# An encoder of a Hyena/GLA layer and an RWKV-7 layer: earlier conditioning, and two value projections in the keys stage

## The chip, the cores and the metric

The kernel runs on one core of a Trainium2 chip (trn2). The metric is the device time of one execution in microseconds (us). Shown before is the median of three runs; one further execution was taken by the hardware profiler, and all rows come from that one.

Engines: PE is TensorE (PEld its weight loads), DVE is VectorE, ACT is ScalarE, POOL is GpSimd, and SP is SyncE, whose queue issues nearly all transfers here.

## The reference

Two layers over a sequence of 256 tokens with 2048 features, all in float32. Each layer has a mixer and a squared-ReLU MLP (2048 to 8192 and back), and each of these four parts ("mix", "f0", "tm", "f1") is conditioned by a vector `c`: `silu(c) @ ada_w + ada_b` gives a shift, a scale and a gate of 2048 numbers each. The first mixer is Hyena beside a gated linear attention; the second ("tm") is RWKV-7 time mixing.

```python
def adaln(x, c, norm_g, ada_w, ada_b):
    m = jax.nn.silu(c) @ ada_w + ada_b
    shift, scale, gate = jnp.split(m[:, None, :], 3, axis=-1)
    return rmsnorm(x, norm_g) * (1.0 + scale) + shift, gate
...
def rwkv7_block(...):
    xx = 0.5 * (hp[:, :-2] + hp[:, 2:]) - h
    xr, xw, xk, xv, xa, xg = [h + xx * mu[j] for j in range(6)]
    r = heads(xr @ w_r); k = heads(xk @ w_k); v = heads(xv @ w_v)
    ...
    for d in range(2):      # both directions: decays, keys, then a scan over the tokens
        ...
        state_out = state_out + o_d
    ...
    return o @ w_o
...
        x = x + gate * y
        h, gate = adaln(x, c, ffn_norm_g[layer], ffn_ada_w[layer], ffn_ada_b[layer])
        x = x + gate * sqrelu_mlp(h, ffn_w1[layer], ffn_w2[layer])
```

The scan is written in chunks of 64 tokens. 32 heads of 64 features make 16 pairs, and four pairs (512 features) a block.

## The kernel before

**Weights.** Every large product is split into three matmuls: a weight tile of 128 x 2 x 512 is loaded by SP (`load`, L488), ACT casts it to a high part and DVE subtracts to get the low part (`split`, L464), and `prod` (L507) issues high x high, high x low and low x high. Each MLP loads 256 such tiles, in the order `w1`, `w2`, `w1`, `w2`, 64 at a time.

**Conditioning as background work.** A third (shift, scale or gate) of one of the four parts is 32 halves. A half is one load of 512 KB into pool `wp` of six tiles (`ada_load`, L313, up to five ahead) and one DVE product with a running sum (`ada_half`, L362). Each weight load adds `rate / 2` to an account, and whenever it reaches one, a half is done (`tick`, L501). In the first MLP the rate is `RF0`, and the account begins at -12. `ada_load` names the order: the current part's gate, then shift and scale of all parts. In the RWKV layer the rate is 0 and the halves are done by `bg_gen` in the loop over pairs; the gate of `tm` is done there, and `spread_gate` spreads it over the partitions at the end of that loop.

**The RWKV layer** (`rwkv`, L1104) has stages. First the six mixes of the input are made; `xk` stays on chip in tiles `xk`, the mixes for `r` and `v` are written to memory and read back, two chunks of 128 features at a time, by `stream` (L999), with a ring of tiles `x`. Second, the keys stage: four rounds over blocks `n`. In each, `rwkv_keys` of four pairs runs in two lanes, woven with the projections `mains`: `k` and `r` of the next blocks, and in round 4 the value block 0. A projection (`rwkv_linear`, L1025) has 16 steps of 12 matmuls, so 192 matmuls, and 8 weight tiles. Value tiles stay on chip. Third, the loop over pairs `p` (L1236): `weave` runs, side by side, the chain of pair `p` (`pair_chain`: four steps, each three rounds of small matmuls with copies by DVE and ACT between), the preparation of the next pair (`pair_prep`), the tail of an earlier one (`pair_tail`), `MT[p]` steps of `main`, the inversion of small triangles, or `BG[p]` conditioning halves. `main` (`work`, L1211) is the rest of the values, blocks 1 to 3, and then the output projection (`rwkv_out`), whose steps wait for finished pairs (`tails`). `M0 + M1` steps of it stand before the first chain: the text calls that stretch the transition. What of the output projection is left follows the last chain.

The order of instructions on each engine's queue is set by a planner with a timeline of its own, within the dependencies and priorities that the program gives; `paced` holds a projection's matmul behind a chain's.

Of the kernel before, what the change touches and what calls it, by code (L numbers as in the profile page):

```python
# [9 lines left out]
F32 = mybir.dt.float32  # L10
# [17 lines left out]
PT = ("0111111", "0111")  # L28
RHY, RGL, RWO, RF0, RF1 = 2.4, 2, 0.6, 1.2, 0.8
HA, HB, HN, HT = 1000, 1000, 0, 0  # L30
LG, MK, XS, TB, DU, RP, IB, L1, MP, AP = 2, 7, 4, 0, -8.0, 1, 3, 0, 3, 5
W1, W2 = 1, 1
BG, IV, CH, MT, B0, B1, M0, M1, LD = (10, 10, 10, 10, 10, 10, 10, 10, 10, 5, 5, 5, 5, 5, 5, 5, 5, 5), 12, 7, (5, 5, 5, 5, 5, 5, 5, 5, 5, 5, 5, 2, 3, 2, 3, 2, 3, 2), 3, 14, 6, 6, 6
PK, PF = 8, 3
RH, ZZ = (0, 2.4, 2, 2), 0
# [178 lines left out]
class Build:  # L214
# [21 lines left out]
    def run(self):  # L236
        nc, ctx, A = self.nc, self.ctx, self.A
        self.const = self.pool(ctx, "const")
        self.wp = self.pool(ctx, "wp", bufs=6)
        self.due, self.rate, self.turn, self.hold, self.starting = 0.0, 0.0, 0, None, False  # L240
        self.cut, self.casts, self.wq = None, [], None
        self.small = self.pool(ctx, "small", bufs=2)
        self.tmp = self.pool(ctx, "tmp", bufs=4)
        self.gstack = ctx.enter_context(ExitStack())
        self.open_gate()
        self.wstack = ctx.enter_context(ExitStack())
        self.open_work()
        self.mm = self.pool(ctx, "mm", bufs=4, space=PSUM)
        self.q = {"sp": nc.sync, "act": nc.scalar, "pool": nc.gpsimd}[QM]
        self.pstack = ctx.enter_context(ExitStack())  # L250
        self.open_ps(4)
        self.xstack = ctx.enter_context(ExitStack())
        self.ada_left = {(s, i): 2 * KT for s in self.stages if s in SUBS for i in range(3)}
        self.ada_next, self.ada_sum, self.ada_out, self.ada_done = [], {}, {}, {}
        self.label = self.stages[0]
        if self.stages[0] != "mix":
            self.start()
            self.load_x()
        for s in SUBS:
            if s in self.stages:  # L260
                self.label = s
                self.rate = RF0 if s == "f0" else RF1
                if s[0] == "f":
                    self.ffn(s)
                elif s == "mix":
                    self.mix()
                else:
                    self.rwkv()
        self.final()
# [43 lines left out]
    def ada_load(self):  # L313

        left, s = self.ada_left, self.label
        todo = [(s, 2)] if not left.get((s, 0)) and not left.get((s, 1)) else []
        if s == "mix" and left.get((s, 0)):
            todo = [(s, 0 if left[s, 0] % 2 or left[s, 0] == left[s, 1] else 1)]
        if self.starting:
            todo = [("mix", i) for i in range(2)] if not todo or todo[0][1] == 2 else todo  # L320
        else:
            todo += [(q, i) for q in SUBS for i in range(2)]
        for u in todo:
            if left.get(u):
                w = self.t(self.wp, [P, D // 2], "w")
                i, j = divmod(2 * KT - left[u], 2)
                self.nc.sync.dma_start(w, self.A["ada_" + u[0]][u[1] * KT + i][:, j])
                left[u] -= 1
                return *u, i, w, j
# [134 lines left out]
    def split(self, a, hi, lo, eng=None):  # L464
        c = self.nc.scalar.copy(hi, a)  # L465
        d = (eng or self.nc.vector).tensor_tensor(lo, a, hi, ALU.subtract)  # L466
        if eng is None:
            self.cut = d.ins
            self.casts = [c.ins]

# [17 lines left out]
    def load(self, name, n, i, pools):  # L488

        self.turn += 1  # L490
        w = self.t(pools[self.turn % len(pools)], [P, 2, NB], "w")
        src = self.A[name][n, i // 2][:, i % 2 * 2 : i % 2 * 2 + 2]
        if self.wq is None:
            self.dma = self.nc.sync.dma_start(w, src).ins
        else:
            with self.tc.issue_after(self.casts[-1]):
                self.wq.dma_start(w, src)
        self.tick(self.rate / 2)
        return w
# [499 lines left out]
    def stream(self, name, n, src, tiles):  # L999
# [4 lines left out]
        def ahead(i):  # L1004
            if isinstance(src, list):
                x = src[i // 4][:, 2 * i % 8 : 2 * i % 8 + 2]
            else:
                x = self.t(self.xt, [P, 2, 2, T], "x", bufs=self.xb, dt=F32R)
                nc.sync.dma_start(x.bitcast(F32), src[:, 2 * i : 2 * i + 2])
            if 2 * (i + PF) < tiles:  # L1010
                w.append(self.load(name, n, i + PF, [self.wp]))
            v = [self.t(self.ws, [P, 2, NB], t, dt=F32R) for t in ("wh", "wl")]
            self.split_weights(w[i], v)
            return x, v
# [89 lines left out]
    def rwkv(self):  # L1104
# [6 lines left out]
        self.ab = [tc.dram_tile([P, 2304 + 8], F32, name=f"ab{p}") for p in range(16)]  # L1111
        self.nd = [tc.dram_tile([P, 2, 1024], F32, name=f"nd{b}") for b in range(4)]
        self.rx = [tc.dram_tile([4, 32, 1024], F32, name=f"rx{b}") for b in range(4)]
        self.rt = [tc.dram_tile([4, 32, 1024], F32, name=f"rt{b}") for b in range(4)]
        self.npt, self.marks, self.tails, self.lag = 0, [], 0, L1
        self.pr = PR
        with ExitStack() as st:
# [4 lines left out]
            nc.vector.tensor_scalar(self.ksc[:, 1, :], self.v("ka"), -0.5, 1.0, ALU.mult, ALU.add)  # L1122
            vp = self.pool(st, "vp", reuse_waits="tile")
            vt = {}

            def values(n, pool):
                def tiles():
                    vt[n] = self.t(pool, [P, 4, T], "v")
                    return vt[n]

                yield from self.rwkv_linear("rw_v", n, 3, tiles)

            st1 = st.enter_context(ExitStack())
            self.open_linear(st1, 3, W1, 3)
            xk = self.pool(st1, "xk", reuse_waits="tile")
            self.xd[2] = [self.t(xk, [P, 8, 2, T], f"xk{i}", dt=F32R) for i in range(2)]
            rk = self.pool(st1, "rk", reuse_waits="tile")
# [15 lines left out]
            mains = [g for n in range(4) for g in (keys(n), self.rwkv_linear("rw_r", n, 0, lambda n=n: kr[n][0]))]  # L1153
            mains = self.in_turn(mains + [values(0, vp)], LD)
            with ExitStack() as st2:
# [11 lines left out]
                self.xstack.close()  # L1167
                self.rate, self.wq = 0.0, None
                mixes = self.spill_mixes(h, xx)
# [5 lines left out]
            with st1:  # L1175
                p1 = self.pool(st1, "p1", reuse_waits="tile")
                for n in range(4):
# [16 lines left out]

                    self.weave((self.take(mains, 34), 34 if n < 3 else 17), (lane(0), 21), (late(), 24), (self.invert(n - 1) if 0 < n <= IB else None, 34))
            with ExitStack() as st1:
                self.open_linear(st1, 2, W2, 3)
                p2 = self.pool(st1, "p2", reuse_waits="tile")
# [12 lines left out]
                def work():  # L1211
                    for n in range(1, 4):
                        yield from values(n, (vp, p2)[n % 2])
                    if PK:
# [10 lines left out]
                def spread_gate(pool):  # L1225
                    r, g = self.need("tm", 2), self.t(pool, [P, 4, T], "v")
                    for i in range(2):
                        self.spread(r, 2 * len(self.gates) + i, g[:, 2 * i : 2 * i + 2, :].rearrange("p a t -> p (a t)"))
                    self.gates.append(g)

                main = work()
                for _ in self.take(main, M0):
                    pass
                self.weave((self.pair_prep(p2, Z[0], vt[0][:, 0, :]), 12), (self.take(main, M1), M1))
                chains, self.gates = {}, []
                for p in range(18):  # L1236
# [3 lines left out]
                    if p < 15:  # L1240
                        nx = self.pair_prep(p2, Z[p + 1], vt[(p + 1) // 4][:, (p + 1) % 4, :])
                    if p == 17:
                        self.npt = None
                        spread_gate(vp)
                    if p < 14:
# [21 lines left out]
                for n in range(4):  # L1267
# [9 lines left out]
                    self.residual("tm", n, pts[n])  # L1277
        self.wq = None
        self.open_gate()
        self.open_work()  # L1280

    def spill_mixes(self, h, xx):
        for j in (2, 0, 3):
            for k in range(0, KT, 2):
# [3 lines left out]
                if j == 2:  # L1288
                    x = self.xd[2][k // 8][:, k % 8 : k % 8 + 2]
                else:  # L1290
                    x = self.t(self.hp, [P, 2, 2, T], "xs", bufs=2, dt=F32R)
# [153 lines left out]
    def pair_load(self, rp, p):  # L1445
        nc = self.nc
        b, pb = p // 4, p % 4
        z = {"p": p}
        z["ar"] = ar = self.t(rp, [P, 2, 2, T], "ar", bufs=2)
        z["bk"] = bk = self.t(rp, [P, 2, 4, P], "bk", bufs=2)  # L1450
# [20 lines left out]

    def pair_prep(self, rp, z, v):

# [4 lines left out]
        X, Tt, N = z["X"], z["T"], z["N"]  # L1478
        z["v"] = v
        z["S"], z["BKT"], z["M"] = {}, [], []  # L1480
# [245 lines left out]
```

## Time and profile before

| | us |
|---|---|
| median of 3 runs | 3051.21 (3048.9 to 3052.1) |
| profiled execution | 3047.34 |
| its span, first to last instruction | 3045.3 |
| first MLP, starts of the first and the last weight split | 648.7 and 1372.5 |
| second MLP, the same (the RWKV layer lies between) | 2300.5 and 3025.8 |

A row of the windows gives, for a stretch of the span, the busy time of each engine with its number of instructions, the granted clock of TensorE as a share of 2.4 GHz, the mean busy share of the 16 DMA engines, and GB/s. A row by line gives line, engine, operation, tiles written and read, shapes, count, busy time, mean of one in ns, and the idle time just before with what ended it. A row of waits says who waited for whom: total, times, longest. Busy time of PE comes from modelled ends of matmuls that overlap.

### The profile page before, as it was taken

To read this page: it belongs to the slowest core of one execution; us is meant where nothing else is said; L and a number is where in the kernel's file an instruction comes from. 1 tells how busy PE (TensorE), PEld (TensorE's weight loads), DVE (VectorE), ACT (ScalarE), POOL (GpSimd) and SP (SyncE) were. 2 spreads that over 40 slices of the span, in tenths; PEclk is the share of its full clock that TensorE was granted. 3 is DMA by queue.
4 is the path that set the end of the run, shared out by engine and by line. 5 is a ranking of instruction groups with operands and counts; after the bars stand their busy time and mean duration, and the time that the engine had idled before them with its cause. 6 is when DMAs were issued, how large, how long until landed. Compare 5 with 4: busy or idle time off the path is not lost. (4 is left out here: it accounts for less than half of the span.)

```text
span 3045.3 us, 52042 instructions
## 1 busy us (share of the span) xinstructions
PE 2871.4 (94%) x20308; PEld 2488.7 (82%) x20308; DVE 2122.1 (70%) x3126; ACT 1301.6 (43%) x1947; POOL 522.2 (17%) x574
## 2 busy tenths in 40 slices
PE   6999989999999999997999878999998999999998
PEld 2678776789988999886888777777778998899986
DVE  7899866657777788787768875775646776455454
ACT  3233334444443444443466542334445443344443
POOL 1211200011100011004354541322322110001000
PEclk9999999999999999998999987999999999999999
DMA  9978777747898988984987788997545777555552
GB/s 328 326 271 284 243 262 263 247 154 244 287 308 306 304 290 290 313 297 158 323 264 249 266 258 226 301 300 208 149 149 194 245 252 272 193 186 183 202 193 93
DMA packets 279970, 752.30 MB, mean 247 GB/s; under 512 B 73081, under 2 KB 99577, under 8 KB 278572
## 3 DMA queue, kind: packets, MB, share of 16 engines
q1 hardware_dynamic: 279148, 745.38, 73.1%
q8 instruction: 159, 2.61, 0.3%
q10 hardware_dynamic: 576, 3.60, 0.3%
q14 instruction: 87, 0.71, 0.1%
HBM read 706.08 MB, written 42.80 MB: 246 GB/s over the span
## 5 line engine op out<-in xcount | busy, mean ns | idle before, releaser
L466 DVE TENSOR_TENSOR f_wl<-f_w,f_wh 128x1024 fp32r<-128x1024 f32 x512 | 630.8, 1233 | 444.3 <-ACT f_wh L465 433.4
L465 ACT CAST f_wh<-f_w 128x1024 fp32r<-128x1024 f32 x512 | 538.0, 1052 | 748.4 <-PE f_mm L512 315.8
L511 PE MATMUL f_mm<-f_h,f_wh 128*128 128x256 f32 x2048 | 579.5, 283 | 0.0
L510 PE MATMUL f_mm<-f_h,f_wh 128*128 128x256 f32 x2048 | 579.5, 283 | 0.0
L512 PE MATMUL f_mm<-f_h,f_wl 128*128 128x256 f32 x2048 | 579.1, 283 | 0.0
L511 PE MATMUL f_mm<-f_wl,f_hid 128*128 128x512 f32 x1024 | 398.6, 389 | 1.1 <-DVE f_wl L466 1.1
L512 PE MATMUL f_mm<-f_wh,f_hid 128*128 128x512 f32 x1024 | 398.5, 389 | 0.0
L511 PEld LDWEIGHTS f_mm<-f_h,f_wh 128*128 128x128 f32 x2048 | 393.2, 192 | 0.1
L510 PEld LDWEIGHTS f_mm<-f_h,f_wh 128*128 128x128 f32 x2048 | 393.0, 192 | 0.1
L512 PEld LDWEIGHTS f_mm<-f_h,f_wl 128*128 128x128 f32 x2048 | 392.9, 192 | 0.0
L510 PE MATMUL f_mm<-f_wh,f_hid 128*128 128x512 f32 x1024 | 357.9, 389 | 0.0
L362 DVE SCALAR_TENSOR_TENSOR mix_w<-mix_w,mix_s 128x1024 f32<-128x1024 f32 x175 | 219.8, 1265 | 77.0 <-DMA mix_w<-in_ada_f 52.5
L466 POOL TENSOR_TENSOR f_hid<-f_u,f_hid 128x512 fp32r<-128x512 f32 x64 | 98.0, 1531 | 990.6 <-ACT f_hid L465 988.2
L362 DVE SCALAR_TENSOR_TENSOR f_w<-f_w,mix_s 128x1024 f32<-128x1024 f32 x174 | 233.6, 1345 | 2.6 <-DMA f_w<-in_ada_f 2.6
L511 PEld LDWEIGHTS f_mm<-f_wl,f_hid 128*128 128x128 f32 x1024 | 192.2, 188 | 41.3 <-DVE f_wl L466 1.7
L512 PEld LDWEIGHTS f_mm<-f_wh,f_hid 128*128 128x128 f32 x1024 | 192.3, 188 | 39.8
L510 PEld LDWEIGHTS f_mm<-f_wh,f_hid 128*128 128x128 f32 x1024 | 192.2, 188 | 39.7
L466 DVE TENSOR_TENSOR tm_wl<-tm_w,tm_wh 128x1024 fp32r<-128x1024 f32 x128 | 164.4, 1287 | 85.8 <-ACT tm_wh L465 81.6
L465 ACT CAST mix_wh<-mix_w 128x1024 fp32r<-128x1024 f32 x114 | 119.4, 1050 | 201.2 <-PE mix_mm L512 86.3
L510 PE MATMUL tm_mm<-tm_x,tm_wh 128*128 128x256 f32 x512 | 161.2, 316 | 12.3 <-DMA tm_x<-mix 10.8
L465 ACT CAST tm_wh<-tm_w 128x1024 fp32r<-128x1024 f32 x128 | 133.4, 1046 | 86.7 <-PE tm_mm L511 60.3
L466 DVE TENSOR_TENSOR mix_wl<-mix_w,mix_wh 128x1024 fp32r<-128x1024 f32 x114 | 142.4, 1254 | 38.8 <-ACT mix_wh L465 38.7
(456 smaller groups left out, 5494.6 us busy)
## 6 DMA issues: line engine op xcount, KB each, us to landing
f_w<-in_w SPq DMA_DIRECT2D x512, 512.0 KB, 5.1
f_w<-in_ada_f SPq DMA_DIRECT2D x125, 512.0 KB, 5.6
mix_w<-in_ada_mix SPq DMA_DIRECT2D x96, 512.0 KB, 6.2
mix_w<-in_w_in SPq DMA_DIRECT2D x80, 512.0 KB, 5.0
mix_w<-in_ada_f SPq DMA_DIRECT2D x64, 512.0 KB, 5.2
tm_x<-mix SPq DMA_DIRECT2D x64, 512.0 KB, 5.8
f_w<-in_ada_tm SPq DMA_DIRECT2D x49, 512.0 KB, 5.8
mix_w<-in_w_out SPq DMA_DIRECT2D x32, 512.0 KB, 4.6
```

Source lines behind the costliest of these rows:

```text
L362: V.scalar_tensor_tensor(w, w, 1.0, self.s[:, j * (D // 2) : (j + 1) * (D // 2)], ALU.mult, ALU.mult, accum_out=a[:, j, i : i + 1])
L465: c = self.nc.scalar.copy(hi, a)
L466: d = (eng or self.nc.vector).tensor_tensor(lo, a, hi, ALU.subtract)
L510: mm(out, lhsT=l[0], rhs=r[0], start=start, stop=False)
L511: mm(out, lhsT=l[0], rhs=r[1], start=False, stop=False)
L512: mm(out, lhsT=l[1], rhs=r[0], start=False, stop=stop)
```

## The change

The gate of `tm` may now be conditioned in the first MLP (`EARLY`), whose rate rises from 1.2 to 1.5. Two value blocks instead of one (`NV`) are projected in the keys stage, in round 4; for them the mix for `v` is loaded once, into tiles that take the places of `xk`. Blocks 2 and 3 stream it as before. Every value block is written to memory, and each pair loads its own part two pairs ahead. The ring of `x` in the pairs' stage has two tiles instead of three. `BG` and `MT` are single numbers, and `VL` is the weight of the projections in round 4. A queue `wq` that was never set is taken out.

```diff
-RHY, RGL, RWO, RF0, RF1 = 2.4, 2, 0.6, 1.2, 0.8
+RHY, RGL, RWO, RF0, RF1 = 2.4, 2, 0.6, 1.5, 0.8
...
-BG, IV, CH, MT, B0, B1, M0, M1, LD = (10, 10, 10, 10, 10, 10, 10, 10, 10, 5, 5, 5, 5, 5, 5, 5, 5, 5), 12, 7, (5, 5, 5, 5, 5, 5, 5, 5, 5, 5, 5, 2, 3, 2, 3, 2, 3, 2), 3, 14, 6, 6, 6
-PK, PF = 8, 3
+BG, IV, CH, MT, B0, B1, M0, M1, LD = 3, 12, 7, 5, 3, 14, 6, 6, 6
+PK, PF, VL, NV, EARLY = 8, 3, 20, 2, (("f0", "tm"),)
...
-            todo += [(q, i) for q in SUBS for i in range(2)]
+            todo += [(q, i) for q in SUBS for i in range(3 if (s, q) in EARLY else 2)]
...
             if isinstance(src, list):
-                x = src[i // 4][:, 2 * i % 8 : 2 * i % 8 + 2]
+                x = src[i]
...
+        self.vd = [tc.dram_tile([P, 4, T], F32, name=f"vd{n}") for n in range(4)]
...
-            self.xd[2] = [self.t(xk, [P, 8, 2, T], f"xk{i}", dt=F32R) for i in range(2)]
+            resident = lambda: [self.t(xk, [P, 2, 2, T], f"xk{i}", dt=F32R) for i in range(KT // 2)]
+            self.xd[2] = resident()
...
-            mains = self.in_turn(mains + [values(0, vp)], LD)
+
+            def values(n, pool):
+                if n == 0:
+                    self.xd[4] = self.xd[3]
+                    spilt, self.xd[3] = self.xd[3], resident()
+                    for i, x in enumerate(self.xd[3]):
+                        nc.sync.dma_start(x.bitcast(F32), spilt[:, 2 * i : 2 * i + 2])
+                v = []
+
+                def tiles():
+                    v.append(self.t(pool, [P, 4, T], "gate", bufs=1 + (pool is not rk)))
+                    return v[0]
+
+                yield from self.rwkv_linear("rw_v", n, 3 if n < NV else 4, tiles)
+                nc.sync.dma_start(self.vd[n], v[0])
+
+            mains = self.in_turn(mains + [values(n, rk) for n in range(NV)], LD)
...
-                    self.weave((self.take(mains, 34), 34 if n < 3 else 17), (lane(0), 21), (late(), 24), (self.invert(n - 1) if 0 < n <= IB else None, 34))
+                    self.weave((self.take(mains, 34 if n < 3 else 17 * NV + 1), 34 if n < 3 else VL), (lane(0), 21), (late(), 24), (self.invert(n - 1) if 0 < n <= IB else None, 34))
             with ExitStack() as st1:
-                self.open_linear(st1, 2, W2, 3)
+                self.open_linear(st1, 2, W2, 2)
...
-                    for n in range(1, 4):
-                        yield from values(n, (vp, p2)[n % 2])
+                    for n in range(NV, 4):
+                        yield from values(n, p2)
...
-                    r, g = self.need("tm", 2), self.t(pool, [P, 4, T], "v")
+                    r, g = self.need("tm", 2), self.t(pool, [P, 4, T], "gate", bufs=2)
...
+        z["v"] = self.t(rp, [P, T], "v", bufs=6)
+        nc.sync.dma_start(z["v"], self.vd[b][:, pb, :])
         z["ar"] = ar = self.t(rp, [P, 2, 2, T], "ar", bufs=2)
...
-    def pair_prep(self, rp, z, v):
+    def pair_prep(self, rp, z):
...
-        z["v"] = v
+        v = z["v"]
```


## Rows read from the trace of the kernel before

**Rows 1.** The page: busy time per engine, then GB/s in 40 slices

```profile
PE 2871.4 (94%) x20308; PEld 2488.7 (82%) x20308; DVE 2122.1 (70%) x3126; ACT 1301.6 (43%) x1947; POOL 522.2 (17%) x574
...
GB/s 328 326 271 284 243 262 263 247 154 244 287 308 306 304 290 290 313 297 158 323 264 249 266 258 226 301 300 208 149 149 194 245 252 272 193 186 183 202 193 93
```

**Rows 2.** Windows of the MLPs: stretch, length, busy (instructions), clock, DMA, GB/s

```profile
840.00:1016.00 176.00, 176.00 (x805) 146.80 (x804) 136.14 (x179) 70.25 (x70) 4.87 (x2) 1.00 0.90 309
1016.00:1200.00 184.00, 184.00 (x1518) 183.22 (x1516) 146.53 (x171) 82.50 (x93) 20.59 (x14) 1.00 0.87 293
1200.00:1374.00 174.00, 174.00 (x789) 144.95 (x788) 137.27 (x175) 72.62 (x80) 2.89 (x2) 1.00 0.88 302
...
2670.00:2854.00 184.00, 184.00 (x1518) 183.26 (x1517) 97.49 (x82) 82.39 (x93) 20.77 (x14) 1.00 0.54 189
2854.00:3027.00 173.00, 173.00 (x783) 144.10 (x783) 91.54 (x84) 72.70 (x79) 2.97 (x2) 1.00 0.46 158
```

**Rows 3.** Windows of the RWKV layer, last a stretch of the second MLP

```profile
1664.00:1745.00 81.00, 71.99 (x590) 65.99 (x589) 65.11 (x118) 46.54 (x90) 38.88 (x49) 0.94 0.80 259
1745.00:1805.00 60.00, 49.19 (x425) 44.58 (x424) 50.37 (x102) 33.66 (x74) 26.80 (x48) 0.91 0.85 271
1805.00:1889.00 84.00, 68.44 (x599) 58.30 (x598) 43.74 (x97) 20.01 (x42) 16.52 (x32) 0.74 0.80 221
1889.00:2045.00 156.00, 149.40 (x1871) 124.84 (x1869) 117.11 (x249) 62.20 (x154) 39.77 (x65) 0.97 0.94 292
2045.00:2203.00 158.00, 156.77 (x2092) 121.27 (x2089) 95.48 (x219) 71.59 (x189) 51.28 (x83) 1.00 0.66 192
2203.00:2292.00 89.00, 86.12 (x601) 64.85 (x598) 46.45 (x76) 41.51 (x78) 23.55 (x22) 1.00 0.44 148
2540.00:2560.00 20.00, 18.88 (x90) 15.47 (x89) 17.32 (x27) 7.49 (x8) 0.00 (x0) 1.00 0.99 387
```

**Rows 4.** Windows of tile wh alone; DVE counts its splits

```profile
1664.00:1745.00 81.00, 51.55 (x248) 41.71 (x247) 18.78 (x16) 15.71 (x15) 0.94 0.80 259
1745.00:1805.00 60.00, 29.35 (x143) 24.32 (x143) 9.26 (x8) 8.26 (x8) 0.91 0.85 271
```

**Rows 5.** Stores of keys stage and pairs: duration min/median/max, first and last start

```profile
L1414 SPq DMA_DIRECT2D ab<-tm_bon x5: 319/374/570, 1745.6 to 1804.5; - x5
...
L1654 SPq DMA_DIRECT2D y_spill<-tm_o x5: 333/383/401, 1916.1 to 2036.7; - x5
...
L1654 SPq DMA_DIRECT2D y_spill<-tm_o x8: 343/550/1160, 2059.3 to 2202.0; - x8
```

**Rows 6.** Conditioning loads (line 327) of the first MLP, with time to landing

```profile
L327 SPq DMA_DIRECT2D f_w<-in_ada_f x93: 327/328/449, 692.6 to 1360.7; - x93
L327 SPq DMA_DIRECT2D f_w<-in_ada_tm x49: 327/328/653, 860.1 to 1081.6; - x49
...
DMA to landing us min/median/max: 3.5/5.7/7.9
```

**Rows 7.** Groups by line, 1374 to 2300 us: the conditioning's products

```profile
L362 DVE SCALAR_TENSOR_TENSOR tm_w<-tm_w,mix_s 128x1024 f32<-128x1024 f32 x35 | 44.1, 1265 | 13.4 <-DMA tm_w<-in_ada_tm 13.1
```

**Rows 8.** Groups by line, 840 to 1374 us: the same line

```profile
L362 DVE SCALAR_TENSOR_TENSOR f_w<-f_w,mix_s 128x1024 f32<-128x1024 f32 x120 | 157.1, 1310 | 2.2 <-DMA f_w<-in_ada_f 2.2
```

**Rows 9.** Windows of line 510 alone, early and late chains

```profile
1889.00:2045.00 156.00, 36.91 (x114) 21.92 (x114) 0.97 0.94 292
2045.00:2203.00 158.00, 25.05 (x58) 10.93 (x58) 1.00 0.66 192
```

**Rows 10.** Waits of PE in the transition, 1805 to 1889 us

```profile
PE tm_mm L510 <- DMA tm_x<-mix: 7.9, 2, 4.9
```

**Rows 11.** Loads of the stored mixes, 1640 to 2100 us

```profile
DMA to landing us min/median/max: 4.6/6.0/10.6
```

More of the change, by code (lines that the diff above doesn't have):

```diff
@@ L240, in run @@
         self.due, self.rate, self.turn, self.hold, self.starting = 0.0, 0.0, 0, None, False
-        self.cut, self.casts, self.wq = None, [], None
+        self.cut = None
         self.small = self.pool(ctx, "small", bufs=2)
@@ L464, in split @@
     def split(self, a, hi, lo, eng=None):
-        c = self.nc.scalar.copy(hi, a)
+        self.nc.scalar.copy(hi, a)
         d = (eng or self.nc.vector).tensor_tensor(lo, a, hi, ALU.subtract)
@@ L468, in split @@
             self.cut = d.ins
-            self.casts = [c.ins]
     def behind(self):
@@ L491, in load @@
         w = self.t(pools[self.turn % len(pools)], [P, 2, NB], "w")
[L492 to L497, printed above, removed]
+        self.dma = self.nc.sync.dma_start(w, self.A[name][n, i // 2][:, i % 2 * 2 : i % 2 * 2 + 2]).ins
         self.tick(self.rate / 2)
@@ L1122, in rwkv @@
             nc.vector.tensor_scalar(self.ksc[:, 1, :], self.v("ka"), -0.5, 1.0, ALU.mult, ALU.add)
[L1123 to L1131, printed above, removed]
             st1 = st.enter_context(ExitStack())
@@ L1167, in rwkv @@
                 self.xstack.close()
-                self.rate, self.wq = 0.0, None
+                self.rate = 0.0
                 mixes = self.spill_mixes(h, xx)
@@ L1233, in rwkv @@
                     pass
-                self.weave((self.pair_prep(p2, Z[0], vt[0][:, 0, :]), 12), (self.take(main, M1), M1))
+                self.weave((self.pair_prep(p2, Z[0]), 12), (self.take(main, M1), M1))
                 chains, self.gates = {}, []
@@ L1240, in rwkv @@
                     if p < 15:
-                        nx = self.pair_prep(p2, Z[p + 1], vt[(p + 1) // 4][:, (p + 1) % 4, :])
+                        nx = self.pair_prep(p2, Z[p + 1])
                     if p == 17:
                         self.npt = None
-                        spread_gate(vp)
+                        spread_gate(p2)
                     if p < 14:
@@ L1277, in rwkv @@
                     self.residual("tm", n, pts[n])
-        self.wq = None
         self.open_gate()
@@ L1288, in spill_mixes @@
                 if j == 2:
-                    x = self.xd[2][k // 8][:, k % 8 : k % 8 + 2]
+                    x = self.xd[2][k // 2]
                 else:
```

## The prediction

> **What bounds the kernel now.** I read the page first: TensorE (PE) is busy 94% of a span of 3045.3 us, VectorE (DVE) 70% [rows 1]. The profiled execution took 3047.34 us in all, 2.0 us of it outside the span and 3.9 us below the median of 3051.21. The sum below is made against 3047.34, and its difference is then put on the median. About 0.2%, 6 us, is what a measurement of this kernel can tell from no change.
>
> An average over three kinds of stage says little, so next come the windows of the stages. In the two MLPs PE is busy without a gap [rows 2]. One `w1` stretch (64 weight tiles) takes 184 us in the first MLP and 184 us in the second; one `w2` stretch takes 174 and 173 us. The first MLP does this with DMA at 0.87 to 0.90 of its time and the second with 0.46 to 0.54. So PE alone sets the pace of the first MLP; its DVE (78%) and its transfers lie beside it. That pace also gives the price of a matmul of 128x256: 184 us for 1518, 0.121 us each, at a granted clock of 1.00.
>
> The RWKV layer has three stages [rows 3]. The keys stage (up to 1805) runs four rounds of four pairs; beside each round stand projection blocks. Round 3, like rounds 1 and 2, has 16 weight splits, two blocks, and takes 81 us; round 4 has 8 splits, one block, and takes 60 us [rows 3, 4]. The last stores of rounds 3 and 4 confirm this: 1745.6 and 1804.5 [rows 5]. PE is idle for 10.8 us of the 60. Then comes a transition (1805 to 1889), in which the second value block is multiplied while PE is idle 15.6 us of 84 and has a granted clock of 0.74, for most of it the lower of the two levels. Last come the chains (1889 to 2203) and the rest of the output projection (to 2292), where PE is busy 149.4 of 156, 156.8 of 158 and 86.1 of 89 us. A pair takes (2036.7-1916.1)/4 = 30.2 us early and (2202.0-2059.3)/7 = 20.4 us later [rows 5].
>
> **The change part by part.**
>
> *Conditioning moved into the first MLP.* The first MLP loads 93 + 49 = 142 halves [rows 6], and the RWKV layer works through 35 more, all in the chains [rows 7]. With RF0 = 1.5 each of its 256 weight loads adds 0.75 to the account, which begins at -12: 256 x 0.75 - 12 = 180 halves, and 142 + 35 = 177 are wanted. All should fit, and nothing is left for the chains. In the MLP this adds 35 x 1.31 = 46 us of DVE [rows 8]. In a `w2` stretch of 176 us that is 64 x 0.15 = 9.6 halves or 13 us more, 149 of 176 us, 85%: still covered by PE. The traffic per weight load grows from 0.524 x 1.6 to 0.524 x 1.75 = 0.918 MB in 2.75 us, that is from a reckoned 305 GB/s (measured 309) to 334. A share of 0.90 for 309 GB/s makes 343 at full share, so the stretch would stand at about 0.97. What covers the transfers is the distance at which loads are issued: six tiles of `wp` at 0.75 + 1/7 tiles per load are 6.7 loads or 18 us ahead, against 5.7 us to landing [rows 6]. I take 0. The lower bound is 0 too, since PE waits for nothing here now. The upper bound: if no more than 328 GB/s came through, as in the best 76 us of the page's slices [rows 1], a load would take 0.918/0.328 = 2.80 us; against 2.72 in the `w2` stretches that is 0.08 us for each of 128 loads, 10 us; I say +12.
>
> *What that frees in the chains.* DVE loses 35 products of 1.265 us, 44.1 us, and 13.1 us in which it stood waiting for their transfers with chain work queued behind it [rows 7]. How much of these 57 us was on the path? Early pairs are 9.8 us longer than late ones. The projection matmuls beside them explain a part: early 3 x 114 of 0.121 us, 41 us in 156; late 3 x 58, nearly all twice as wide, some 38 us in 158 [rows 9], that is 8.0 us per early pair and 4.9 per late one. Clock explains about 1 us per pair (0.97 of 156 us). There remain some 5.7 us over five pairs, 28 us, for DVE, its waits and transfers at 0.94 of the time. Bounds 0 and -28. I take -10, nearer to nothing, because PE shows only 6.6 us of idle time in the 156.
>
> *One value block out of the chains, one more into the keys stage.* A block is 192 matmuls, 192 x 0.121 = 23 us of PE. Before, block 0 runs in round 4, block 1 in the transition, 2 and 3 in the chains; after, 0 and 1 run in round 4, 2 in the transition, 3 in the chains. Round 4 then has what rounds 2 and 3 have: 81 - 60 = +21 us. The lower bound is 23 - 10.8 = +12, if all its idle PE time is filled; the upper is +23. I take +20. The chains lose 23 us of PE work; where PE is that full the time falls by as much: -23. Bounds: -5 (if the wait between steps, not PE, sets the pace) and -23. The transition keeps one block, with its second-half `x` streamed through two buffers where there were three; PE waited 7.9 us there for `tm_x` [rows 10], which lands in 6.0 us [rows 11]. I put 0, bounds 0 and +5.
>
> *The input held on chip, the trip of the values through memory, the rest.* Blocks 0 and 1 share one load of 8 tiles instead of two, 4.2 MB less. The tiles take the places of the keys' input, so the eight loads wait for the last key block and come as one burst; behind them on SP's queue stand round 4's loads. 4.2 MB at that round's 271 GB/s are 15 us of transfer for a block that is needed at once only in its first tile: 0, bound +3. Four stores and 16 loads of values are added and 35 + 8 loads fall away, at 0.33 us of SP each [rows 6]; the queue gets shorter, and each load is issued two pairs (over 40 us) ahead: 0. BG and MT as constants and VL change only how the filling work is spread. The gate's spreading stays at the end.
>
> Sum: 0 - 10 + 20 - 23 = -13 us on 3047.34, about 3034; on the median 3038.
>
> **A rule against the reading.** The windows show weight loads busy 124.8 of 156 and 121.3 of 158 us in the chains, and 183.2 of 184 us in the `w1` stretch [rows 2, 3]. The Trainium skill (Perfetto Trace Analysis, "Identifying the Most-Contended Engine") says that matmul busy time is a poor measure of how near PE is to its limit and that the busy share of weight loads is a better one. By that rule the chains have a fifth of PE to spare. Its result is rival 1, and the rows do not exclude it.
>
> **Rivals.** *1, slower: the chains are set by their own steps.* If each pair is a sequence of small matmuls with copies between, and projection matmuls only fill gaps, then taking a block out gives the lower end, -5, and clearing DVE gives nothing, while round 4 still pays +20: +15, 3066 us. It decides once the pairs stay at 30 us early after the block is gone. For it: the 80% of weight loads. Against it: late pairs of 20 us, with PE idle 1.2 of 158.
>
> *2, no change: the first MLP becomes bound by its transfers.* Its +12 cancels most of the -13: 3050 us. For it: a share of 0.97 to come. Against it: 20 us of the second MLP show 387 GB/s [rows 3]. The Trainium skill (HBM Reference, "Specifications (TRN2)") gives some 358 GB/s as a core's share and about 425 for a core that streams alone; the 387 agree with the second.
>
> *3, much faster: DVE and the transfers set the early pairs.* Then the -28 comes whole, and round 4 fills its idle time: -28 + 14 - 23 = -37, 3014 us. For it: 13.1 us of DVE waiting on a transfer, ahead of chain work, and DMA at 0.94. Against it: PE's own idle time of 6.6 us.
>
> *4: it doesn't do what it says.* Instructions are placed by a planner, and the second block already had its weights loaded before 1805; if round 4 just pushes it out again, or conditioning is left over, about 0 to -5 remains: 3048.
>
> **How the numbers follow.** Forecast 0.40 (its own range 3026 to 3048), rival 1 0.18, rival 2 0.14, rival 3 0.20, rival 4 0.08. Faster by over 0.2%: 0.38 of the forecast, 0.20 of rival 3, 0.02 of rival 4, 0.60. Within 0.2%: 0.02, 0.02 of rival 1, 0.08 of rival 2 and 0.04 of rival 4, 0.16. The rest, 0.24, is slower. The range goes from rival 3's 3014, less 2, to rival 1's 3066; it leaves out the upper half of rival 1 and the far ends of the others.
>
> **What would show it.** Right: no conditioning loads between 1380 and the second MLP; 177 in the first MLP with PE still without a gap and stretches of 174 to 184 us; a fourth round of about 80 us; early pairs of 22 to 26 us; the RWKV layer shorter by some 13 us. Wrong: PE waiting on `f_w` in the first MLP (rival 2), early pairs still at 30 us (rival 1), early pairs at 20 us (rival 3), or a fourth round far over 81 us because of the burst of loads.

## The result, and the profile after

The changed kernel takes 3035.6 us (median of five, 3027.6 to 3043.9) against 3051.2: a ratio of 0.995, 95% interval 0.9937 to 0.9963, or 11 to 19 us less. The forecast was 3038. Its profiled execution is the slowest of the five, 3043.93 us with a span of 3042.2. Part of that lies ahead of everything that was changed: the first MLP begins at 653.2 us where it began at 648.7, and over all profiles of this study at 646.8 to 655.0. So stages are compared below, not spans. Ratios leave out two executions that took more than twice the time of the others (6831 us in E3, 11674 us of the kernel before beside E9 to E12).

The windows of the first MLP after (stretch, length, busy time of PE, PEld, DVE, ACT and POOL with their instructions, clock, DMA, GB/s), and PE's waits in it:

```profile
845.00:1021.00 176.00, 176.00 (x802) 146.71 (x801) 143.46 (x190) 70.00 (x70) 2.89 (x2) 1.00 0.94 333
1021.00:1204.00 183.00, 183.00 (x1512) 182.34 (x1511) 154.84 (x191) 81.77 (x92) 20.45 (x14) 1.00 0.91 320
1204.00:1378.00 174.00, 174.00 (x790) 144.98 (x789) 144.88 (x194) 72.88 (x80) 2.95 (x2) 1.00 0.93 327
```

```profile
PE f_ps L439 <- issue: 4.5, 1, 4.5
```

```profile
L362 DVE SCALAR_TENSOR_TENSOR f_w<-f_w,mix_s x177: 1207/1218/2329, 720.2 to 1374.8; 128x1024 f32<-128x1024 f32 x177
```

These answer to [rows 2]: the stretches are as long as before, now with 333, 320 and 327 GB/s and 143 to 155 us of DVE. PE's one wait stands at the start, where it also stood before. The last row counts the products of the halves in this MLP: all 177 are done here, the gate of `tm` among them.

The windows of the RWKV layer after, for [rows 3]; then the stores, for [rows 5]; then value block 1 alone (reads from the tiles `xk`) and block 2 (reads from the ring `x`):

```profile
1669.00:1749.00 80.00, 73.18 (x601) 67.46 (x601) 65.49 (x118) 46.42 (x90) 32.32 (x47) 0.94 0.89 297
1749.00:1807.00 58.00, 52.44 (x459) 48.55 (x459) 49.97 (x98) 34.35 (x77) 28.59 (x48) 0.94 0.70 216
1807.00:1913.00 106.00, 83.94 (x823) 74.48 (x822) 56.44 (x123) 32.68 (x55) 19.94 (x36) 0.86 0.86 263
1913.00:2062.00 149.00, 143.33 (x1901) 116.91 (x1899) 76.67 (x177) 62.63 (x166) 38.20 (x70) 0.97 0.68 192
2062.00:2225.00 163.00, 157.20 (x2021) 119.26 (x2021) 93.56 (x211) 74.03 (x192) 47.78 (x81) 0.98 0.54 156
2225.00:2290.00 65.00, 60.20 (x369) 45.43 (x370) 31.29 (x52) 26.87 (x49) 15.44 (x14) 0.93 0.40 127
```

```profile
L1415 SPq DMA_DIRECT2D ab<-tm_bon x6: 371/449/1667, 1748.7 to 1806.6; - x6
...
L1657 SPq DMA_DIRECT2D y_spill<-tm_o x5: 382/550/554, 1933.4 to 2027.9; - x5
...
L1657 SPq DMA_DIRECT2D y_spill<-tm_o x9: 382/400/552, 2043.8 to 2230.7; - x9
```

```profile
1792.00:1820.00 28.00, 25.61 (x192) 24.58 (x192) 0.00 (x0) 0.00 (x0) 0.96 0.67 207
...
1829.00:1901.00 72.00, 31.43 (x192) 28.61 (x192) 0.00 (x0) 0.00 (x0) 0.00 (x0) 0.81 0.84 258
```

Round 4 (1749 to 1807) is no longer than before though it has a block more, and DMA in it is at 0.70. The 192 matmuls of block 1 run from 1792 to 1820, mostly behind it and with hardly a pause; block 2 then takes 72 us in the transition. The first tail store comes at 1933.4 where it came at 1916.1. Early pairs take (2027.9-1933.4)/4 = 23.6 us instead of 30.2, late ones (2230.7-2043.8)/8 = 23.4 instead of 20.4, where more of the output projection now stands beside them (E3 and E8 below show this shift). The stores do not bracket equal work: between the first and the fifth PE carries out 1427 matmuls before and 1209 after, so these times are signs, and not the gain.

So that all runs can be compared, this table gives the lengths in us in the profile of each: the first MLP; from its last weight split to the last `bon` store (the keys stage); from there to the first tail store; from the first to the last of the 14 tail stores; from there to the first split of the second MLP; and the sum of the last four. One profile stands for each, so a few us of difference say nothing: the profile after shows the layer only 6.1 us shorter, where the medians differ by 15.6.

| kernel | first MLP | keys | to first tail | tails | rest | RWKV layer | ratio of times to before (95%) |
|---|---|---|---|---|---|---|---|
| before | 725.0 | 432.0 | 111.6 | 304.7 | 79.7 | 928.0 | 1 |
| after | 724.4 | 430.2 | 126.8 | 297.3 | 67.5 | 921.9 | 0.9950 (0.9937 to 0.9963) |
| E1 conditioning alone | 724.5 | 429.3 | 114.3 | 290.4 | 79.8 | 913.8 | 0.9952 (0.9935 to 0.9969) |
| E2 values alone | 725.7 | 433.4 | 133.9 | 302.9 | 65.6 | 935.7 | 1.0019 (1.0004 to 1.0034) |
| E3 one block ahead | 724.4 | 428.6 | 118.6 | 308.5 | 65.2 | 920.9 | 0.9975 (0.9962 to 0.9987) |
| E4 VL = 35 | 724.5 | 450.0 | 106.1 | 288.8 | 66.6 | 911.5 | 0.9954 (0.9936 to 0.9972) |
| E5 E1 + 65 products | 724.4 | 429.8 | 119.3 | 314.4 | 81.7 | 945.2 | 1.0059 (1.0047 to 1.0072) |
| E6 E1 + 65 loads | 724.5 | 433.6 | 110.8 | 321.4 | 81.4 | 947.1 | 1.0030 (1.0018 to 1.0042) |
| E7 RF0 = 2.0 | 748.8 | 431.1 | 128.3 | 288.4 | 67.4 | 915.1 | 1.0028 (1.0017 to 1.0040) |
| E8 E3, old MT | 724.6 | 427.8 | 119.4 | 291.8 | 79.8 | 918.8 | 0.9970 (0.9959 to 0.9982) |
| E9 E1 + 35 products | 725.5 | 429.3 | 122.9 | 297.2 | 81.7 | 931.2 | 1.0011 (1.0000 to 1.0022) |
| E10 E1 + 35 loads | 725.4 | 428.7 | 111.0 | 308.6 | 81.7 | 930.0 | 1.0005 (0.9995 to 1.0015) |
| E11 E1, ring of two | 724.8 | 431.9 | 122.1 | 281.9 | 79.8 | 915.7 | 0.9957 (0.9943 to 0.9972) |
| E12 input streamed | 724.4 | 433.9 | 130.0 | 287.4 | 64.9 | 916.2 | 0.9970 (0.9957 to 0.9983) |

### The profile page after: what moved, and what is told of

It reads as the page before. It is cut to its first block, busy times and chain, and to the rows that moved or that the text cites. A ratio compares the mean times of both kernels' runs of the same rounds, so it can differ in the third digit from the quotient of the medians.

```text
span 3042.2 us, 52049 instructions
## 1 busy us (share of the span) xinstructions
PE 2855.6 (94%) x20308; PEld 2477.4 (81%) x20308; DVE 2111.1 (69%) x3126; ACT 1302.9 (43%) x1947; POOL 509.0 (17%) x574
## 5 line engine op out<-in xcount | busy, mean ns | idle before, releaser
L362 DVE SCALAR_TENSOR_TENSOR f_w<-f_w,mix_s 128x1024 f32<-128x1024 f32 x209 | 275.0, 1317 | 1.7 <-DMA f_w<-in_ada_f 1.7
L465 ACT CAST mix_wh<-mix_w 128x1024 fp32r<-128x1024 f32 x114 | 119.4, 1050 | 204.3 <-PE mix_mm L506 88.9
L504 PE MATMUL tm_mm<-tm_x,tm_wh 128*128 128x256 f32 x384 | 119.0, 311 | 13.7 <-DMA tm_x<-mix 13.4
```

Of the source, the lines that this page charges most:

```text
L362: V.scalar_tensor_tensor(w, w, 1.0, self.s[:, j * (D // 2) : (j + 1) * (D // 2)], ALU.mult, ALU.mult, accum_out=a[:, j, i : i + 1])
L504: mm(out, lhsT=l[0], rhs=r[0], start=start, stop=False)
```

## The experiments

**E1, the conditioning alone**, on the kernel before:

```diff
-RHY, RGL, RWO, RF0, RF1 = 2.4, 2, 0.6, 1.2, 0.8
+RHY, RGL, RWO, RF0, RF1 = 2.4, 2, 0.6, 1.5, 0.8
-            todo += [(q, i) for q in SUBS for i in range(2)]
+            todo += [(q, i) for q in SUBS for i in range(3 if (s, q) == ("f0", "tm") else 2)]
```

> The kernel before with the gate's conditioning in the first MLP alone (RF0 1.5 and the longer list of thirds); the values stay as they were. Theory A (the prediction's sum): the chains lose 35 products and their transfers, about -10 us, 0.997 of before, with early pairs some 2 us shorter and the first MLP as long as before within 2 us. Theory B (PE alone sets the chains, the conditioning is covered in either place): no change, 1.000 within 0.001. Theory C (the conditioning is the whole of the gain): -15 us, 0.995.

Measured: 3035.82 us beside 3049.57 for before, a ratio of 0.9952. That is theory C: one line and one rate give as much as the whole change. The layer is 14.2 us shorter, all of it in the tails (304.7 to 290.4). Windows of the chains in E1, as in [rows 3]; its early stores; then the whole stretch from the last `bon` store to the last tail store, of the kernel before and of E1:

```profile
1889.00:2045.00 156.00, 156.00 (x2097) 132.33 (x2095) 84.72 (x196) 67.50 (x167) 39.94 (x73) 0.98 0.75 218
2045.00:2203.00 158.00, 156.23 (x2043) 119.63 (x2043) 90.70 (x211) 73.02 (x196) 49.14 (x81) 1.00 0.56 156
```

```profile
L1654 SPq DMA_DIRECT2D y_spill<-tm_o x6: 320/382/559, 1920.7 to 2041.7; - x6
```

```profile
1804.50:2220.70 416.20, 392.22 (x4786) 317.48 (x4786) 264.25 (x584) 162.12 (x409) 113.75 (x188) 0.93 0.78 230
1806.40:2211.10 404.70, 386.39 (x4786) 314.12 (x4785) 219.67 (x503) 161.79 (x409) 107.42 (x188) 0.93 0.68 191
```

In the same 156 us (1889 to 2045) PE carries out 2097 matmuls where it had carried out 1871, its busy time going from 149.4 to 156.0. An eighth more matmuls fit into 4% more busy time: what looked like a nearly full PE was not. The last two rows hold the work equal: the same 4786 matmuls, at the same clock, take 11.5 us less, and half of that (392.2 to 386.4) is busy time. The early pairs take (2041.7-1920.7)/5 = 24.2 us; over as many stores the kernel before takes (2059.3-1916.1)/5 = 28.6.

**E2, the values alone**, on the changed kernel:

```diff
-RHY, RGL, RWO, RF0, RF1 = 2.4, 2, 0.6, 1.5, 0.8
+RHY, RGL, RWO, RF0, RF1 = 2.4, 2, 0.6, 1.2, 0.8
-BG, IV, CH, MT, B0, B1, M0, M1, LD = 3, 12, 7, 5, 3, 14, 6, 6, 6
+BG, IV, CH, MT, B0, B1, M0, M1, LD = (10, 10, 10, 10, 10, 10, 10, 10, 10, 5, 5, 5, 5, 5, 5, 5, 5, 5), 12, 7, 5, 3, 14, 6, 6, 6
-PK, PF, VL, NV, EARLY = 8, 3, 20, 2, (("f0", "tm"),)
+PK, PF, VL, NV, EARLY = 8, 3, 20, 2, ()
```

> The changed kernel with the conditioning put back (RF0 1.2, empty EARLY, BG as before): two value blocks ahead, one shared input, values through memory. Theory A: about -3 to -5 us against before, 0.999. Theory B: the whole -15 us, 0.995. Theory C: 0 to +5 us, 1.000 to 1.002.

Measured: 1.0019 (1.0004 to 1.0034), some 6 us slower than before, theory C again. The first tail store comes 22 us later than before after round 4, and the shorter rest (65.6 for 79.7) does not make up for it. By the medians E1 and E2 do not add up to the whole: -14.6 and +5.8 would be -9, and the whole is -15. The three intervals together leave room for this gap, so it is not shown that the two parts act on each other. With the conditioning out of the chains, the values cost nothing that can be measured (0.9950 beside E1's 0.9952). Where the 6 us of E2 arise was not settled.

**E3, one block ahead instead of two**, and **E8, the same with the old pace**:

```diff
-PK, PF, VL, NV, EARLY = 8, 3, 20, 2, (("f0", "tm"),)
+PK, PF, VL, NV, EARLY = 8, 3, 20, 1, (("f0", "tm"),)
```

> The changed kernel with NV = 1: one value block ahead as before, its input in tiles, values through memory, conditioning in the first MLP. Theory A (the second block costs the transition what it saves the chains, apart from some 3 to 5 us): -10 to -12 us against before, 0.996 to 0.997; first tail store some 15 us earlier than in the changed kernel. Theory B: about 0, 1.000. Theory C: -15 us, 0.995.

> E3 (one value block ahead, values through memory) with MT as it was before, so that late pairs take 2 or 3 steps of the projection instead of 5. E3 was some 7 us slower than E1. If the late pace is the cause: 0.995 to 0.996, late pairs (from the seventh to the last) back from 213 to 195 us and the tail back from 65 to 80 us, with a smaller sum. If the trip of the values through memory and the smaller ring are the cause: 0.997 to 0.998 again, the sum of late pairs and tail unchanged at 275 to 279 us.

E8 has, besides, `MT = (5, 5, 5, 5, 5, 5, 5, 5, 5, 5, 5, 2, 3, 2, 3, 2, 3, 2)`. Measured: 0.9975 and 0.9970, nearest to theory A. The pace only shifts time between the tails and the rest: 308.5 + 65.2 = 373.7 and 291.8 + 79.8 = 371.6 us. Both sit 5 to 7 us above E1 (E3, run in the same set, is clear of E1, medians 3042.6 and 3035.8; E8 is not beyond its interval), more than half of it on the way to the first tail store: 118.6 and 119.4 us for 114.3, with 933, 934 and 932 matmuls. So the rest of the value part costs those 5 to 7 us with one block ahead, and the second block takes them back. PE's waits in that stretch, in E3 and then in E8, show one that E1 cannot have, since its values stay on chip:

```profile
PE tm_ps L1490 <- DMA tm_v<-vd: 5.6, 1, 5.6
PE tm_ps L1490 <- DMA tm_v<-vd: 5.9, 1, 5.9
```

In E3 the first pair's values are asked for at 1808.8, behind other loads on SP's queue, when PE has already stood idle since 1806.4; it goes on at 1812.0. PE's waits for transfers in this stretch come to 13.8 us in E1, 17.8 in E3 and 20.2 in E8. In the changed kernel the wait for `tm_v` is 1.8 us, since more work stands ahead of the first pair.

**E11, E1 with the ring of the value input cut to two tiles**:

```diff
-                self.open_linear(st1, 2, W2, 3)
+                self.open_linear(st1, 2, W2, 2)
```

> E1 with the ring of the mix for the values cut from three tiles to two in the pairs' stage, as the change has it. If the ring is what made E3 and E8 some 6 us slower than E1: 0.997, with the first chain of the pairs starting some 5 us later after round 4 than in E1. If it is the trip of the values through memory or the tiles of the shared input: 0.995 as E1.

Measured: 0.9957, as E1. The first tail store does come later after round 4 (122.1 for 114.3 us), but 1089 matmuls stand in that stretch instead of 932, and the tails are as much shorter. PE's waits for `tm_x` there are 7.4 us with two tiles and 8.5 with three. So the ring shows no cost, though the interval would leave room for some 6 us. That leaves the trip of the values through memory, whose wait has the size of the loss, the tiles of the shared input, and small edits that came with them (the weight of the projections in round 4 is 20 for 17); no run takes one of these away alone.

**E4, both value blocks spread over round 4**:

```diff
-PK, PF, VL, NV, EARLY = 8, 3, 20, 2, (("f0", "tm"),)
+PK, PF, VL, NV, EARLY = 8, 3, 35, 2, (("f0", "tm"),)
```

> The changed kernel with VL = 35 in place of 20, so that both value blocks are spread over round 4 and none is left behind it. If the second block is placed behind round 4 because its steps are dealt out slowly, and the first pair's loads wait for it there: round 4 grows from 57 us to 70 to 80 us, the stretch from its last store to the first tail store shrinks from 127 us to about 105 us, and the time is the same as the changed kernel's or up to 8 us less. If the first pair waits for something else (the last inversions, the loads' own time): round 4 grows, the stretch stays near 127 us and the time is 10 to 20 us more.

Measured: 0.9954, as the changed kernel. Its stores, to be held against those after (last `bon` 1806.6, first tail store 1933.4):

```profile
L1415 SPq DMA_DIRECT2D ab<-tm_bon x6: 371/575/869, 1747.4 to 1825.0; - x6
...
L1657 SPq DMA_DIRECT2D y_spill<-tm_o x14: 320/547/1688, 1931.2 to 2220.0; - x14
```

The first of the six stores (1747.4) belongs to the end of round 3 and the last to that of round 4, which now takes 1825.0 - 1747.4 = 77.6 us where the changed kernel took 1806.6 - 1748.7 = 57.9. The last `bon` store comes that much later, and the stretch to the first tail store falls to 106.1: both as expected of a block that is dealt out slowly and then stands in the first pair's way. Set against E1, which leaves the blocks where they were, the keys stage is 20.7 us longer and the rest of the layer 484.5 - 461.5 = 23.0 us shorter. But E1 also lacks the trip through memory and the shared input. E3 has them and differs from E4 in `NV` and `VL` alone: against it the keys stage is 21.4 us longer and the rest 492.3 - 461.5 = 30.8 us shorter, 4.5 us of that the wait for `tm_v` (1.1 for 5.6). In time E4 is some 7 us below E3 (medians 3035.3 and 3042.6 of one set, clear of noise). So the block costs in the keys stage what the forecast said, and saves somewhat more where it leaves; E1, without the rest of the value part, is as fast as both together.

**E12, the value input streamed** instead of held on chip (the loads into tiles in `values` taken out, so that `rwkv_linear` reads memory):

```diff
-                    spilt, self.xd[3] = self.xd[3], resident()
-                    for i, x in enumerate(self.xd[3]):
-                        nc.sync.dma_start(x.bitcast(F32), spilt[:, 2 * i : 2 * i + 2])
```

> The changed kernel with the shared input taken back: both value blocks of round 4 stream the mix from memory, 4.2 MB more, through the ring of three. If holding the input on chip is what lets the second block run in 28 us behind round 4: that block takes 40 to 65 us, as the one in the transition does, the first tail store comes 10 to 20 us later, and the time is 5 to 15 us over the changed kernel, 0.997 to 1.000. If its loads would have been hidden anyway: 0.995.

Measured: 0.9970 (0.9957 to 0.9983), some 6 us over the changed kernel with intervals that overlap at their ends. Block 1 takes 36 us (1796 to 1832) where it took 28, PE waits 4.1 us for `tm_x`, and the first tail store comes 130.0 us after round 4 for 126.8. The direction is the first theory's, but the block's 36 us and the 3 us of delay are less than it said (40 to 65, and 10 to 20). Whether all 6 us come from there is open: in its one profile the layer is even shorter than in that of the changed kernel (916.2 for 921.9).

**E5 and E6, one half of the conditioning put back into E1's chains.** E5 has the products without loads, E6 the loads without products; what they make is not used. In place of the background halves stand:

```diff
+            w, a = self.t(self.wp, [P, D // 2], "w"), self.t(self.small, [P, 2], "tot")
+            self.nc.vector.scalar_tensor_tensor(w, self.s[:, : D // 2], 1.0, self.s[:, D // 2 :], ALU.mult, ALU.mult, accum_out=a[:, :1])
...
+            w = self.t(self.wp, [P, D // 2], "w")
+            self.nc.sync.dma_start(w, self.A["ada_tm"][2 * KT + i % KT][:, j])
```

> E1 (conditioning in the first MLP alone) with 35 products of the same shape put back into the pairs' loop, on data that is on chip already, so without their loads; they compute nothing that is used. If the gain of E1 came from DVE's time, ahead of the chains' copies: +8 to +14 us over E1, 0.998 to 1.000 of before, with the early pairs back near 133 us for five. If it came from the loads (DVE waiting on them, SP's queue, the full DMA): +0 to +3 us, 0.995 to 0.996.

> E1 with the 35 loads of 512 KB put back into the pairs' loop, and no products; what they bring is not used. If the gain of E1 came from the loads: +8 to +14 us over E1, 0.998 to 1.000. If it came from DVE's time or from DVE waiting for a landing: +0 to +3 us, 0.995 to 0.996.

Measured: 1.0059 and 1.0030, some 33 and 24 us over E1. The expectations say 35, but the kernels issued 65 each, five to ten at each of twelve pairs, so they show only that either half has a price. **E9 and E10** have 35, at the pairs where the kernel before had them (10, 10, 10, 5):

> As E5, but with the dose and the place of before: 35 products, 10 each at the fourth to sixth pair and 5 at the seventh (E5 held 65, five or ten at each of twelve pairs: 0.48 us for each). If a product costs the chains 0.4 to 0.5 us wherever it stands: +14 to +17 us over E1, 0.9998 to 1.001 of before. If the dose of E5 was what made DVE tight (its late pairs grew most): +5 to +9 us, 0.997 to 0.998.

> As E6, but with 35 loads in the place of before (E6 held 65, 0.37 us for each). If a load costs as much wherever it stands: +13 us over E1, 0.9995. If E6 cost by its dose alone: +3 to +6 us, 0.996 to 0.997. Products and loads together, as in the kernel before, cost 14.6 us over E1; were each the whole of its sum, they would have to overlap nearly wholly.

Measured: 1.0011 (1.0000 to 1.0022) and 1.0005 (0.9995 to 1.0015), 18 and 16 us over E1. Each half alone costs as much as both did in the kernel before (14.6), within the intervals. Of E9: its products by line (none has a transfer to wait for) and its windows, then a wait of ACT from 1890 to 2050 in E9 and the same one in E1; of E10: its windows, then waits of PE and of ACT from 1890 to 2050:

```profile
L353 DVE SCALAR_TENSOR_TENSOR tm_w<-mix_s 128x1024 f32<-128x1024 f32 x35 | 43.4, 1245 | 0.2
...
1889.00:2045.00 156.00, 149.84 (x1853) 124.17 (x1850) 118.70 (x247) 62.51 (x154) 48.47 (x65) 1.00 0.69 202
2045.00:2203.00 158.00, 156.70 (x2062) 121.13 (x2061) 90.73 (x209) 71.09 (x188) 47.29 (x82) 1.00 0.58 162
...
ACT tm_Q L1579 <- DVE tm_Q L1578: 15.1, 14, 2.8
ACT tm_Q L1573 <- DVE tm_Q L1572: 9.5, 10, 1.8
```

```profile
1889.00:2045.00 156.00, 146.72 (x1907) 124.51 (x1903) 78.79 (x182) 62.82 (x157) 36.19 (x66) 0.97 0.93 289
2045.00:2203.00 158.00, 155.45 (x1980) 119.85 (x1980) 88.59 (x201) 69.62 (x182) 46.62 (x80) 0.98 0.68 192
...
PE tm_mm L518 <- ACT tm_wh L473: 7.0, 1, 7.0
...
ACT tm_wh L473 <- DMA tm_w<-in_rw_v: 12.1, 4, 5.2
```

The rows point to two different ways. In E9, DMA is at 0.69, below E1's 0.75, and DVE is busy 118.7 of 156 us where E1 had 84.7: the small copies of the chains stand in DVE's queue among 43.4 us of products, and ACT waits 15.1 us for those of `tm_Q` (9.5 in E1, 22.9 in the kernel before). In E10, DVE has less to do than in E1, but ACT waits 12.1 us for the projection's own weights (E1's ACT has no such wait in that stretch, the kernel before 5.5 us), and PE then 7.0 us for ACT, in one wait; the other 9 of its 16 us stand in no single row. Loads and weights share the six tiles of `wp`, SP's queue and the DMA engines; which of the three makes the weights late was not tried apart, and neither was what E9's use of `wp` tiles adds. The planner also orders every queue anew for each kernel, which no run here holds fixed. So the two prices are shown, and the ways are read from the rows.

**E7, a still faster rate in the first MLP**: `RF0 = 2.0` in the changed kernel.

> The changed kernel with RF0 = 2.0: the same 177 halves, done in some 190 weight loads instead of 252, so 1.05 MB of traffic per load. With 343 GB/s at full DMA share (309 at 0.90) a load of the w2 stretch would take 3.06 us for 2.75 and one of w1 3.06 for 2.87: the first MLP grows by 30 to 40 us, PE waiting for f_w. If the 387 GB/s of the short stretch hold for long, DVE at 2.62 us per 2.75 us is next and the first MLP grows by 0 to 8 us.

Measured: 1.0028, the first MLP 24.4 us longer, between the two expectations. Windows of its four stretches (`w1` from 701 on, `w2`, `w1`, `w2`), waits of PE and of ACT in the whole MLP:

```profile
701.00:850.00 149.00, 145.84 (x1199) 143.95 (x1198) 130.42 (x185) 65.50 (x77) 16.97 (x12) 1.00 0.94 336
850.00:1034.00 184.00, 178.12 (x776) 142.64 (x775) 158.90 (x225) 67.08 (x68) 3.71 (x2) 1.00 0.98 365
1034.00:1226.00 192.00, 187.69 (x1522) 185.31 (x1521) 170.59 (x232) 81.24 (x92) 22.43 (x14) 0.99 0.95 348
1226.00:1398.00 172.00, 172.00 (x774) 142.97 (x773) 88.78 (x83) 72.28 (x79) 2.90 (x2) 1.00 0.55 187
...
PE f_mm L506 <- DVE f_wl L466: 4.9, 9, 1.3
PE f_mm L504 <- ACT f_wh L465: 4.7, 8, 1.3
...
PE f_mm L505 <- DVE f_wl L466: 3.5, 7, 0.5
...
ACT f_wh L465 <- DMA f_w<-in_w: 93.5, 25, 7.6
```

While the halves last, the `w2` stretch runs at 365 GB/s with DMA at 0.98 and takes 184 us for 176, and ACT waits 93.5 us for weights (53.0 in the changed kernel, where PE feels none of it). PE waits 4.9 + 4.7 + 3.5 = 13.1 us for ACT and DVE; the other 11 us are in no row of waits. In the last stretch, with the halves used up, all is as before. So a limit such as rival 2's is there. The 334 GB/s of the change stay under it; E7 asks for some 381 (1.05 MB per 2.75 us) and gets 365. That the transfers set it is the nearer reading (DMA at 0.98, DVE busy 158.9 of 184 us), but no run slows one of the two alone.

## Why the prediction was right, and where it was not

The range and the direction held, and 3038 is 2.4 us from the median. That it came so near is in part luck: the forecast took -10 for the conditioning, -3 for the second block and 0 for the rest of the value part, and the runs give some -15, -7 and +5 to +7, misses that cancel. Its steps fared unequally.

*Conditioning in the first MLP, 0:* right in size and reason. 334 GB/s were reckoned for the `w2` stretch and 333 measured, 149 us of DVE and 143 to 145 measured, the MLP's length the same (725.0, 724.4). DMA stood at 0.94, not at the reckoned 0.97. E7 shows that this was not free by a wide margin.

*What it frees in the chains, -10:* right in direction, mis-sized: E1 gives -14.6. The step's reason for staying nearer to nothing, that PE showed only 6.6 us of idle time in 156, was the fault: E1 put an eighth more matmuls into the same time. The other end, 28 us, came from stores that bracket unequal work. The Trainium skill (Perfetto Trace Analysis, "Identifying the Most-Contended Engine") holds the busy share of weight loads to be the better measure of how near PE is to its limit. The trace agrees with it in direction: 124.8 of 156 us left a fifth to spare, and E1 raised it to 132.3. The prediction had turned that into rival 1, in which the chains are set by their own steps, and concluded that clearing DVE would then give nothing; but E9's products on DVE alone cost those steps 18 us.

*How the halves cost:* the prediction put both under one sum, DVE's 44.1 us of products and 13.1 of waiting. E9 and E10 show two costs of 16 to 18 us that lie over each other, and the second, of loads alone, had no term: the working names the transfers at 0.94, but prices only DVE's products and waits.

*One block into round 4, +20, and out of the chains, -23:* wrong in place. In the changed kernel round 4 did not grow; the block was left behind it and put off the first pair. Where the block is really woven into round 4 (E4), the two terms come out at +20.7 and -23.0 against E1, and at +21.4 and -30.8 against E3, which lacks the second block alone; there the move gains some 7 us instead of 3. In time, E1, E4 and the changed kernel cannot be told apart (0.9952, 0.9954, 0.9950): what the second block gains, the rest of the value part takes.

*The input held on chip, the trip through memory, the smaller ring, 0:* the ring shows no cost (E11). The trip and the shared tiles together cost 5 to 7 us with one block ahead (E3, E8), and holding the input gains perhaps 6 with two (E12). The step's reason, that each load is issued two pairs ahead, fails for the first pair, which has none before it: there PE waits 5.6 and 5.9 us in E3 and E8, and 1.8 in the changed kernel.

Rival 3 had the right cause, DVE and the transfers in the early pairs, at -28; half of that was there. (Its sum takes 14 for round 4, where the prediction's own lower bound is 12.) Rival 4's worry, that the block is pushed out of round 4, came true and cost little. No run here was faster than the changed kernel beyond its interval.

## What to carry to other kernels

Here background work was worth moving out of a stage of small dependent steps into one that another engine fills, as long as that stage did not grow; find out how much it takes by raising the rate until it does. Before a saving is split over "the compute" and "the loads" of such work, put each back alone: here either half cost the whole, so removing only one gained nothing that could be measured (E9 and E10). Moving a block of PE's work from one stage to another cost its own time where it went (21 us); what the move gains must be read against a kernel that differs in the block alone (some 7 us, against E3), and not against one that also lacks what comes with it.

## What was not expected of the hardware

PE can be shown busy for 149.4 of 156 us with 1871 matmuls and for 156.0 us with 2097, and the same 4786 matmuls for 392.2 or 386.4 us: in these stretches of small dependent matmuls its busy time is not its load. And DMA's busy share does not scale with its rate: 309 GB/s at 0.90 led to a reckoned 343 at full share, while 184 us of E7 ran at 365 GB/s and 0.98.
